# One whole-array state product in a chunked scan, its outputs gathered into one group per head pair, and two heads taken in turn

## The chip, the cores and the metric

The kernel runs on one core of a Trainium2 chip. Five engines work from queues of their own: TensorE (PE; its weight loads are listed as PEld), VectorE (DVE), ScalarE (ACT), GpSimd (POOL) and SyncE (SP), which issues the DMAs. The metric is the device time of one execution in microseconds; lower is better.

## The reference

A decoder block over 512 tokens and 1024 channels. The part that the change touches is the RWKV-7 recurrence, here for 8 heads of 64 channels:

```python
def step(state, inp):
    r_t, w_t, k_t, v_t, a_t, b_t = inp
    sa = jnp.einsum('bhvk,bhk->bhv', state, a_t)
    state = state * w_t[:, :, None, :] + sa[..., None] * b_t[:, :, None, :] + v_t[..., None] * k_t[:, :, None, :]
    y = jnp.einsum('bhvk,bhk->bhv', state, r_t)
    return state, y
```

Around it stand a projection to all branches (`u = h @ w_in`), a stick-breaking attention branch, sigmoid gates that merge both branches, an output projection, a squared-ReLU MLP and a gated embedding. All of it is float32.

## The kernel before

Large products are split into high and low parts, three matmuls for one (`mm3`, L191 to L193: 128x512 each). A "unit" is one block of weights, 8 such triples.

The program falls into stages. First comes attention, until about 176 us. Then the recurrence is worked in chunks of 64 tokens, two heads (a head pair `hp`) at a time, with 64 channels of one head on partitions 0 to 63 and of the other on 64 to 127. `prepare(hp)` makes everything of a pair that needs no state: scores within chunks (L778), the inverse of a triangular matrix by 32x32 and 64x64 pieces (L808 to L892), and transposes. `scan(hp)` then goes through the 8 chunks in order. In each chunk L919 multiplies the state `S` (both heads on the diagonal of a 128x128 tile), DVE adds it to `UV0` (L920), L928 makes the product for the next state, one matmul per head, L940 the output within the chunk, one per head, and ACT copies that output to `y` (L941); DVE (L936) forms the next `S`. After 8 chunks a normalisation of `y` follows on DVE and ACT (L953 to L960), then transposes and the gate (L965, L970).

The loop over `st` drives `prepare(st)`, `scan(st - 1)` and a list of filler units (`FILL[st]`, `mm3` products of other branches) together: `drive` takes steps of them in turn by the counts given. A scheduler then puts each engine's instructions in a fixed order; what an engine meets first in that order, it waits for. So a pair's scan runs beside the next pair's `prepare` in the stages of 208 to 360 us, and the last scan runs beside filler alone, until about 413 us. Behind it stand the up projection, output projection, MLP and embedding stages.

A matmul names rows of the array by the partitions of its inputs and columns by the partitions of its output: L928 and L940 read 128 rows and fill 64 columns, L778 reads 64 rows and fills 128 columns, L881 is 64 by 64, L871 32 by 32; L919 and the filler use the whole array. The profile shows each float32 matmul of a small product as two MATMUL instructions.

Of the kernel before, what the change touches and what calls it, by code (L numbers as in the profile page):

```python
# [14 lines left out]
ALU = mybir.AluOpType  # L15
# [3 lines left out]
P = 128  # L19
# [4 lines left out]
C = 64  # L24
NC = T // C
CP = NC // 2
# [59 lines left out]
def tile_block(ctx: ExitStack, tc: tile.TileContext, xT, xt, pT, wts, lora, cols_d, gfin_d, consts_d, out, dbg=None):  # L86
    nc = tc.nc
    act, dve, pool, pe, sync = nc.scalar, nc.vector, nc.gpsimd, nc.tensor, nc.sync

    HALVES = (slice(0, 64), slice(64, 128))  # L90
# [181 lines left out]
    with ExitStack() as sA:  # L272
# [43 lines left out]
        with ExitStack() as s1:  # L316
# [12 lines left out]
            ps = ps_z()  # L329
# [197 lines left out]
            for _ in islice(v, 1):  # L527
# [6 lines left out]
                              op0=ALU.mult, op1=ALU.add)  # L534
# [37 lines left out]
        with ExitStack() as s2:  # L572
# [22 lines left out]
            def ps_gen():  # L595
                return ps2.tile([P, T], F32, name="ps_g", bufs=3)
# [26 lines left out]
            def ps_chain():  # L623
                return ps2.tile([P, T], F32, name="ps_c", bufs=2)
# [56 lines left out]
            def prepare(hp, got):  # L681
# [90 lines left out]
                for g in range(2):  # L772
                    yield
                    pss = [ps_gen() for _ in range(2)]
                    for c in range(4):
                        cp, q = g * 2 + c // 2, c % 2
                        for hh, sl in enumerate(HALVES):
                            pe.matmul(pss[hh][:, c * P:(c + 1) * P], BK[sl, 2 * cp + 1 - q, :, :].rearrange("p s t -> p (s t)"),  # L778
                                      Q[sl, cp, 1 + 2 * q:3 + 2 * q, :], start=True, stop=True)
                    for hh in range(2):  # L780
                        ps4 = pss[hh].rearrange("p (cp s t) -> p cp s t", cp=2, s=4)
                        pk = slice(hh * 4 + 2 * g, hh * 4 + 2 * g + 2)
                        dve.tensor_tensor(out=LM[:, pk], in0=ps4[:, :, 1:3, :],
                                          in1=strict.rearrange("p (o u t) -> p o u t", o=1, u=1).broadcast_to([P, 2, 2, C]),
                                          op=ALU.mult)
                        dve.tensor_tensor(out=DE[:, hh, g * 4:g * 4 + 4, :].rearrange("p (cp q) t -> p cp q t", q=2),
                                          in0=ps4[:, :, 0::3, :],
                                          in1=incl.rearrange("p (o u t) -> p o u t", o=1, u=1).broadcast_to([P, 2, 2, C]),
                                          op=ALU.mult)
# [77 lines left out]
                ps = ps_gen()  # L867
                ps3 = ps[:, 0:256].rearrange("p (k x) -> p k x", k=8)
                for k in range(8):
                    for r in (0, 2):  # L870
                        pe.matmul(ps3[QUADS[r], k], Yc[QUADS[r + 1], k, :], Z[QUADS[r + 1], k, QUADS[r + 1]], start=True, stop=True)  # L871
                for r in (0, 2):
                    act.copy(out=Z[QUADS[r], :, QUADS[r + 1]], in_=ps3[QUADS[r]])
                yield
# [2 lines left out]
                for cp in range(CP):  # L877
                    for hh in range(2):
                        j = cp * 2 + hh
                        for q, (own, oth) in enumerate((HALVES, HALVES[::-1])):  # L880
                            pe.matmul(ps[own, j * C:(j + 1) * C], LM[oth, hh * 4 + cp, q, :], Vt[oth, cp, hh * C:(hh + 1) * C],  # L881
                                      start=True, stop=True)
                act.copy(out=MA[:, :, 0:C], in_=ps.rearrange("p (j x) -> p j x", j=8))
                yield
                UV0 = p2.tile([P, CP, 2, C], F32, name="UV0", tag="mid", bufs=NMID)
# [18 lines left out]
            def scan(hp, got):  # L904

                csl = slice(hp * P, (hp + 1) * P)
                Q, DE, UV, UV0, BKt, gc_, bon = (got[n] for n in ("Q", "DE", "UV", "UV0", "BKt", "gc_", "bon"))
                y = p2.tile([P, CP, P], F32, name="y", tag="gn", bufs=2)
                S = None
                for c in range(NC):  # L910
                    yield
                    cp, q = c // 2, 1 - c % 2
                    half, oth = HALVES[q], HALVES[1 - q]
                    psu = ps_chain()
                    if S is None:
                        pool.tensor_copy(out=UV[half, cp, q, :], in_=UV0[half, cp, :, :].rearrange("p h x -> p (h x)"))
                    else:

                        pe.matmul(psu[:, 0:P], Q[:, cp, 4 * q:4 * q + 2, :].rearrange("p s t -> p (s t)"), S, start=True, stop=True)  # L919
                        dve.tensor_tensor(out=UV[half, cp, q, :], in0=psu[half, 0:P],  # L920
                                          in1=UV0[half, cp, :, :].rearrange("p h x -> p (h x)"), op=ALU.add)
                    if c < NC - 1:
                        gc = gc_[:, c:c + 1]
                        ps = ps2.tile([P, T], F32, name="ps_s", bufs=1)
                        Sn = Sb[hp % 2 * 3 + c % 3]
                        for hh in range(2):
                            sl = HALVES[hh]
                            pe.matmul(ps[sl, 0:C], BKt[:, c, sl], UV[:, cp, q, sl], start=True, stop=True)  # L928
                        if S is None:
                            for sl in HALVES:  # L930
                                dve.tensor_scalar(out=Sn[sl, sl], in0=ps[sl, 0:C], scalar1=gc[sl], scalar2=None, op0=ALU.mult)
                        else:
                            Sg = p2.tile([P, C], F32, name="Sg", bufs=4)
                            for sl in HALVES:
                                pool.tensor_scalar(out=Sg[sl], in0=S[sl, sl], scalar1=gc[sl], scalar2=None, op0=ALU.mult)
                                dve.scalar_tensor_tensor(out=Sn[sl, sl], in0=ps[sl, 0:C], scalar=gc[sl], in1=Sg[sl],  # L936
                                                         op0=ALU.mult, op1=ALU.add)
                    for hh in range(2):
                        sl = HALVES[hh]
                        pe.matmul(psu[oth, sl], DE[:, hh, 2 * cp + q, :], UV[:, cp, q, sl], start=S is None, stop=True, skip_group_check=True)  # L940
                    act.copy(out=y[oth, cp, :], in_=psu[oth, 0:P])  # L941
                    if c < NC - 1:
                        S = Sn

                yield

                y3 = y.rearrange("p c (h x) -> p (c h) x", h=2)
                st = p2.tile([P, 4, 8], F32, name="st", bufs=2)

                def each(i):  # L950
                    return st[:, i, :].rearrange("p (j o) -> p j o", o=1).broadcast_to([P, 8, C])

                dve.tensor_reduce(out=st[:, 0, :], in_=y3, axis=mybir.AxisListType.X, op=ALU.add)  # L953
                dve.scalar_tensor_tensor(out=y3, in0=each(0), scalar=-1.0 / C, in1=y3, op0=ALU.mult, op1=ALU.add)
# [25 lines left out]
            for st in range(HP + 1):  # L980
                parts = [(len(FILL[st]) * KT, filling(FILL[st]))]
                if st < HP:
                    parts.append((28, prepare(st, got[st])))
                if st > 0:
                    parts.append((11, scan(st - 1, got[st - 1])))
                drive(*parts)


# [363 lines left out]
```

## Time and profile before

| | us |
|---|---|
| median of 3 runs | 879.9 (879.37 to 880.65) |
| the profiled execution | 881.98 |
| its span | 880.1 |
| PE busy | 860.2 (98%) |
| DVE busy | 676.5 (77%) |
| ACT busy | 452.9 (51%) |

The span is the time from the first to the last instruction of the profiled execution; 1.9 us lie around it. Busy time is a union of the instructions' durations. Matmuls are pipelined, each listed from its issue to its end, so what a matmul costs PE is read from the distance between starts, not from its duration.

### The profile page before, as it was taken

The numbers are of one execution on the slowest core, as the hardware profiler recorded it, in microseconds if no ns is written. First come the engines' busy times: TensorE is split into PE (matmuls) and PEld (weight loads), VectorE is DVE, ScalarE is ACT, GpSimd is POOL, SyncE is SP. The second block draws the span as 40 slices with busy tenths as digits, with TensorE's granted clock in tenths as the row PEclk, the third lists the DMA queues.
The fourth block names the chain that finished last, engine by engine and source line by source line (L and its number), as shares of the span: only waits on it lengthen the run. The fifth ranks groups of instructions, "written<-read, shape, count | busy, mean of one in ns | idle before, by whom it ended". The sixth has DMA issues, their size and how long they took to land.

```text
span 880.1 us, 13611 instructions
## 1 busy us (share of the span) xinstructions
PE 860.2 (98%) x5238; PEld 692.7 (79%) x5238; DVE 676.5 (77%) x1230; ACT 452.9 (51%) x730; POOL 87.3 (10%) x136
## 2 busy tenths in 40 slices
PE   8999999999999999999999999999999999999995
PEld 5778787877777777777888888888888888888885
DVE  6899987896979889456853789857975987697666
ACT  6788887734445254424523555334534543453743
POOL 1332421002302141120000000000000000000000
PEclk9999999999999999999999999999999999999998
DMA  7212212121211315238934820631252034200422
GB/s 266 97 48 73 72 61 90 66 97 50 72 50 49 109 64 173 89 132 273 307 103 135 294 73 4 202 128 50 72 189 98 25 122 165 96 1 1 168 72 96
DMA packets 32272, 95.32 MB, mean 108 GB/s; under 512 B 3664, under 2 KB 3664, under 8 KB 32208
## 3 DMA queue, kind: packets, MB, share of 16 engines
q1 hardware_dynamic: 32208, 94.46, 31.7%
q8 instruction: 41, 0.67, 0.3%
q14 instruction: 23, 0.19, 0.1%
HBM read 83.96 MB, written 10.49 MB: 107 GB/s over the span
## 4 chain that ended last, share of the span: by engine, by line
PE 77%; DVE 11%; ACT 6%; DMA 3%; issue 2%; SPq 0%; ACTq 0%; DVEq 0%
PE ps_m L191 14%; PE ps_m L192 14%; PE ps_m L193 14%; PE ps_m L206 7%; PE ps_m L208 7%; PE ps_m L207 7%; DMA w_raw<-in_wts_dram 2%; DVE w_lo L176 1%; ACT hx L1025 1%; PE ps_o L492 1%; DMA tmp<-gates 1%; PE ps_g L778 1%; PE ps_g L808 1%; PE ps_g L892 1%; PE ps_z L500 1%
## 5 line engine op out<-in xcount | busy, mean ns | idle before, releaser
L175 ACT CAST w_hi<-w_raw 128x1024 fp32r<-128x1024 f32 x94 | 98.9, 1053 | 150.2 <-PE ps_m L192 93.4
L176 DVE TENSOR_TENSOR w_lo<-w_raw,w_hi 128x1024 fp32r<-128x1024 f32 x94 | 115.3, 1226 | 37.2 <-ACT w_hi L175 36.5
L191 PE MATMUL ps_m<-h_hi,w_hi 128*128 128x512 f32 x320 | 131.3, 412 | 1.6 <-ACT w_hi L221 1.4
L192 PE MATMUL ps_m<-h_lo,w_hi 128*128 128x512 f32 x320 | 128.5, 402 | 0.3 <-DVE h_lo L349 0.3
L193 PE MATMUL ps_m<-h_hi,w_lo 128*128 128x512 f32 x320 | 128.2, 400 | 0.0
L191 PE MATMUL ps_m<-hx,w_hi 128*128 128x512 f32 x256 | 99.8, 390 | 0.4 <-ACT hx L1025 0.4
L192 PE MATMUL ps_m<-hx,w_hi 128*128 128x512 f32 x256 | 99.7, 390 | 0.0
L193 PE MATMUL ps_m<-hx,w_lo 128*128 128x512 f32 x256 | 99.6, 390 | 0.0
L191 PEld LDWEIGHTS ps_m<-h_hi,w_hi 128*128 128x128 f32 x320 | 60.6, 189 | 13.8 <-ACT w_hi L221 1.9
L193 PEld LDWEIGHTS ps_m<-h_hi,w_lo 128*128 128x128 f32 x320 | 60.2, 188 | 12.3
L192 PEld LDWEIGHTS ps_m<-h_lo,w_hi 128*128 128x128 f32 x320 | 60.4, 189 | 12.0 <-DVE h_lo L349 1.3
L191 PEld LDWEIGHTS ps_m<-hx,w_hi 128*128 128x128 f32 x256 | 48.0, 188 | 10.5 <-ACT hx L1025 0.6
L192 PEld LDWEIGHTS ps_m<-hx,w_hi 128*128 128x128 f32 x256 | 48.1, 188 | 10.1 <-DVE hx L1026 0.2
L193 PEld LDWEIGHTS ps_m<-hx,w_lo 128*128 128x128 f32 x256 | 48.1, 188 | 9.9
L208 PE MATMUL ps_m<-w_hi,fS 128*128 128x512 f32 x128 | 49.8, 389 | 0.0
L206 PE MATMUL ps_m<-w_hi,fS 128*128 128x512 f32 x128 | 49.8, 389 | 0.0
L207 PE MATMUL ps_m<-w_lo,fS 128*128 128x512 f32 x128 | 49.8, 389 | 0.0
L208 PE MATMUL ps_m<-w_hi,fA 128*128 128x512 f32 x96 | 37.4, 389 | 0.0
L206 PE MATMUL ps_m<-w_hi,fA 128*128 128x512 f32 x96 | 37.4, 389 | 0.0
L207 PE MATMUL ps_m<-w_lo,fA 128*128 128x512 f32 x96 | 37.4, 389 | 0.0
L221 ACT CAST fS<-sums 128x256 fp32r<-128x256 f32 (+1 forms) x32 | 19.8, 620 | 33.3 <-DVE sums L1117 33.3
L1190 DVE TENSOR_TENSOR xs<-ps_m,xs 128x512 f32<-128x512 f32 x56 | 35.9, 682 | 0.0
(378 smaller groups left out, 1900.2 us busy)
## 6 DMA issues: line engine op xcount, KB each, us to landing
w_raw<-in_wts_dram SPq DMA_DIRECT2D x98, 512.0 KB, 3.5
gates<-gg SPq DMA_DIRECT2D x16, 256.0 KB, 2.0
x_in<-in_xT_dram SPq DMA_DIRECT2D x8, 256.0 KB, 6.1
tmp<-gates SPq DMA_DIRECT2D x8, 256.0 KB, 3.3
upsb<-tmp SPq DMA_DIRECT2D x8, 256.0 KB, 3.2
ga<-upsb SPq DMA_DIRECT2D x8, 256.0 KB, 6.1
gb<-gates SPq DMA_DIRECT2D x8, 256.0 KB, 6.3
xs<-in_xt_dram SPq DMA_DIRECT2D x4, 512.0 KB, 6.9
```

The lines of the kernel that those rows point to most:

```text
L175: act.copy(out=hi, in_=raw)
L176: dve.tensor_tensor(out=lo, in0=raw, in1=r32(hi), op=ALU.subtract)
L191: pe.matmul(ps, wh, xh[:, k, t], start=first, stop=False)
L192: pe.matmul(ps, wh, xl[:, k, t], start=False, stop=False)
L193: pe.matmul(ps, wl, xh[:, k, t], start=False, stop=last)
L206: pe.matmul(ps, xh[:, k + j], wh, start=first and j == 0, stop=False, skip_group_check=True)
L207: pe.matmul(ps, xh[:, k + j], wl, start=False, stop=False, skip_group_check=True)
L208: pe.matmul(ps, xl[:, k + j], wh, start=False, stop=last and j == 1, skip_group_check=True)
L221: act.copy(out=hi, in_=src)
L492: pe.matmul(ps_o[:, j * P:T], vv[:, j, hh, :, :].rearrange("p a d -> p (a d)"), part[:, ZB[j]:ZB[j] + ZN[j]], start=j == 2 and part is wh, ...
L500: pe.matmul(zt[b][:, :n], tri, part[:, s:s + n], start=False, stop=False, skip_group_check=True)
L1190: dve.tensor_tensor(out=xb, in0=pss[t2], in1=xb, op=ALU.add)
```

## The change

The two state matmuls of a chunk (one per head) become one over all 128 rows and 128 columns, of which the two diagonal 64x64 blocks are used. The outputs within chunks leave the chunk loop: two PSUM banks `psy`, one for odd and one for even chunks, hold the state's part of all chunks, and after the loop 16 matmuls add to them in one group, odd and even chunk in turn; two ACT copies then fetch `y`. The scores are issued in an order that is fixed, one head after the other (`tc.issue_after`), as are the pieces of L871 before those of L881.

```diff
-                        for hh, sl in enumerate(HALVES):
-                            pe.matmul(pss[hh][:, c * P:(c + 1) * P], BK[sl, 2 * cp + 1 - q, :, :].rearrange("p s t -> p (s t)"),
-                                      Q[sl, cp, 1 + 2 * q:3 + 2 * q, :], start=True, stop=True)
+                        for hh in (1, 0):
+                            sl = HALVES[hh]
+                            with tc.issue_after(last.ins) if last else nullcontext():
+                                last = pe.matmul(pss[hh][:, c * P:(c + 1) * P], BK[sl, 2 * cp + 1 - q, :, :].rearrange("p s t -> p (s t)"),
+                                                 Q[sl, cp, 1 + 2 * q:3 + 2 * q, :], start=True, stop=True)
...
-                    for r in (0, 2):
-                        pe.matmul(ps3[QUADS[r], k], Yc[QUADS[r + 1], k, :], Z[QUADS[r + 1], k, QUADS[r + 1]], start=True, stop=True)
+                    for r in (2, 0):
+                        last = pe.matmul(ps3[QUADS[r], k], Yc[QUADS[r + 1], k, :], Z[QUADS[r + 1], k, QUADS[r + 1]], start=True, stop=True)
...
-                            pe.matmul(ps[own, j * C:(j + 1) * C], LM[oth, hh * 4 + cp, q, :], Vt[oth, cp, hh * C:(hh + 1) * C],
-                                      start=True, stop=True)
+                            with tc.issue_after(last.ins):
+                                pe.matmul(ps[own, j * C:(j + 1) * C], LM[oth, hh * 4 + cp, q, :], Vt[oth, cp, hh * C:(hh + 1) * C],
+                                          start=True, stop=True)
...
+                psy = [ps_chain() for _ in range(2)]
                 for c in range(NC):
...
-                    psu = ps_chain()
+                    psu = psy[c % 2][:, cp * P:(cp + 1) * P]
...
-                        pe.matmul(psu[:, 0:P], Q[:, cp, 4 * q:4 * q + 2, :].rearrange("p s t -> p (s t)"), S, start=True, stop=True)
+                        pe.matmul(psu, Q[:, cp, 4 * q:4 * q + 2, :].rearrange("p s t -> p (s t)"), S, start=c in (1, 2), stop=True,
+                                  skip_group_check=True)
...
-                        for hh in range(2):
-                            sl = HALVES[hh]
-                            pe.matmul(ps[sl, 0:C], BKt[:, c, sl], UV[:, cp, q, sl], start=True, stop=True)
+                        pe.matmul(ps[:, 0:P], BKt[:, c, :], UV[:, cp, q, :], start=True, stop=True)
...
-                    for hh in range(2):
-                        sl = HALVES[hh]
-                        pe.matmul(psu[oth, sl], DE[:, hh, 2 * cp + q, :], UV[:, cp, q, sl], start=S is None, stop=True, skip_group_check=True)
-                    act.copy(out=y[oth, cp, :], in_=psu[oth, 0:P])
...
+                for cp in range(CP):
+                    for hh, sl in enumerate(HALVES):
+                        for odd in (1, 0):
+                            with tc.issue_after(last.ins) if last else nullcontext():
+                                last = pe.matmul(psy[odd][HALVES[odd], cp * P + hh * C:cp * P + (hh + 1) * C], DE[:, hh, 2 * cp + 1 - odd, :],
+                                                 UV[:, cp, 1 - odd, sl], start=False, stop=True, skip_group_check=True)
+                for odd in range(2):
+                    act.copy(out=y[HALVES[odd]], in_=psy[odd].rearrange("p (c x) -> p c x", c=CP)[HALVES[odd]])
```

How the order on PE moves, at three places. In the changed kernel L919 is L926, L928 is L935, L940 is L953, L778 is L782, L871 is L875, L881 is L886 and L965 is L977. The order counts a float32 matmul once. First, PE in one chunk of the last scan, before:

```order
L919 MATMUL ps_c<-S_1573,Q 128x128
L191 MATMUL ps_g<-osb,w_hi 128x512
L192 MATMUL ps_g<-osb,w_hi 128x512
L193 MATMUL ps_g<-osb,w_lo 128x512
L191 MATMUL ps_g<-osb,w_hi 128x512
L928 MATMUL ps_s<-UV,BKt 64x64 x2
L940 MATMUL ps_c<-UV,DE 64x64 x2
```

and the same chunk in the changed kernel:

```order
L926 MATMUL ps_c<-S_1573,Q 128x128
L191 MATMUL ps_g<-osb,w_hi 128x512
L192 MATMUL ps_g<-osb,w_hi 128x512
L193 MATMUL ps_g<-osb,w_lo 128x512
L191 MATMUL ps_g<-osb,w_hi 128x512
L935 MATMUL ps_s<-UV,BKt 128x128
```

As many filler matmuls stand between the state's two products as before; the four 64-column matmuls have become one. At the end of each scan now stands one row `L953 MATMUL ps_c<-UV,DE 64x64 x16`, which in the last scan 41 filler matmuls follow before L977.

Second, PE at the scores of the second head pair, before:

```order
L764 MATMUL ps_g<-cst,Q 128x128 x4
L778 MATMUL ps_g<-Q,BK 128x128 x16
L919 MATMUL ps_c<-S_1568,Q 128x128
L192 MATMUL ps_m<-h_lo,w_hi 128x512
L193 MATMUL ps_m<-h_hi,w_lo 128x512
```

and now:

```order
L764 MATMUL ps_g<-cst,Q 128x128 x4
L782 MATMUL ps_g<-Q,BK 128x128
L192 MATMUL ps_m<-h_lo,w_hi 128x512
L926 MATMUL ps_c<-S_1568,Q 128x128
L193 MATMUL ps_m<-h_hi,w_lo 128x512
L191 MATMUL ps_m<-h_hi,w_hi 128x512
L782 MATMUL ps_g<-Q,BK 128x128 x8
L935 MATMUL ps_s<-UV,BKt 128x128
L192 MATMUL ps_m<-h_lo,w_hi 128x512
L193 MATMUL ps_m<-h_hi,w_lo 128x512
L191 MATMUL ps_m<-h_hi,w_hi 128x512
L192 MATMUL ps_m<-h_lo,w_hi 128x512
```

The 16 score matmuls stood in one row; now they stand in three, of 1, 8 and 7, with whole-array work between. Within a row the two heads now alternate; before, four of one head often followed each other.

Third, PE at the end of the triangular inverse of that pair, before:

```order
L871 MATMUL ps_g<-Z,LX 32x32
L881 MATMUL ps_g<-Vt,LM 64x64 x4
L871 MATMUL ps_g<-Z,LX 32x32 x15
L881 MATMUL ps_g<-Vt,LM 64x64 x12
L965 MATMUL ps_c<-cst,y 128x128 x4
```

and now:

```order
L875 MATMUL ps_g<-Z,LX 32x32 x16
L886 MATMUL ps_g<-Vt,LM 64x64 x16
L193 MATMUL ps_m<-h_hi,w_lo 128x512
L191 MATMUL ps_m<-h_hi,w_hi 128x512
L192 MATMUL ps_m<-h_lo,w_hi 128x512
L977 MATMUL ps_c<-cst,y 128x128
```

The 64x64 matmuls no longer stand between the 32x32 ones.

## Rows read from the trace of the kernel before

**Rows 1.** Page, part 1: busy us (share of the span) x instructions of each engine.

```profile
PE 860.2 (98%) x5238; PEld 692.7 (79%) x5238; DVE 676.5 (77%) x1230; ACT 452.9 (51%) x730; POOL 87.3 (10%) x136
```

**Rows 2.** Busy time by stretch, the stages of the scan: us, busy of each engine, clock, DMA.

```profile
208.00:260.00 52.00, 51.32 (x571) 39.28 (x570) 45.00 (x114) 24.63 (x47) 13.38 (x16) 1.00 0.18 62
260.00:312.00 52.00, 51.52 (x569) 39.73 (x565) 44.51 (x115) 23.66 (x46) 10.75 (x16) 1.00 0.20 67
312.00:360.00 48.00, 46.60 (x533) 35.46 (x532) 41.28 (x106) 23.55 (x42) 11.45 (x13) 1.00 0.41 133
360.00:402.00 42.00, 41.97 (x228) 32.66 (x227) 21.34 (x39) 12.22 (x21) 7.96 (x13) 1.00 0.38 126
```

**Rows 3.** Timeline of PE in one chunk of the last scan: start us, us, what.

```profile
380.77 0.39 PE L193 MATMUL ps_m<-h_hi,w_lo 128*128 128x512 f32 x1
381.00 0.38 PE L919 MATMUL ps_c<-S,Q 128*128 128x128 f32 x2
...
381.45 0.39 PE L192 MATMUL ps_m<-h_lo,w_hi 128*128 128x512 f32 x1
...
381.92 0.39 PE L191 MATMUL ps_m<-h_hi,w_hi 128*128 128x512 f32 x1
382.24 0.34 PE L928 MATMUL ps_s<-UV,BKt 128*64 128x64 f32 x4
382.41 0.40 PE L940 MATMUL ps_c<-UV,DE 128*64 128x64 f32 x4
382.74 0.50 PE L192 MATMUL ps_m<-h_lo,w_hi 128*128 128x512 f32 x1
383.08 0.40 PE L193 MATMUL ps_m<-h_hi,w_lo 128*128 128x512 f32 x1
```

**Rows 4.** Groups of PE instructions by line: count, busy us, mean ns, idle before.

```profile
L940 PE MATMUL ps_c<-UV,DE 128*64 128x64 f32 x128 | 12.9, 224 | 0.0
L928 PE MATMUL ps_s<-UV,BKt 128*64 128x64 f32 x112 | 9.7, 246 | 0.4 <-DVE UV L920 0.3
```

**Rows 5.** Timeline of PE at the last chunk, which has no state product.

```profile
402.23 0.39 PE L191 MATMUL ps_g<-osb,w_hi 128*128 128x512 f32 x1
...
402.55 0.45 PE L940 MATMUL ps_c<-UV,DE 128*64 128x64 f32 x4
...
403.26 0.39 PE L193 MATMUL ps_g<-osb,w_lo 128*128 128x512 f32 x1
```

**Rows 6.** L778 alone in two stretches of the first pair's scores.

```profile
178.62:179.17 0.55, 0.55 (x4) 0.55 (x5) 1.00 0.72 291
179.17:180.18 1.01, 1.01 (x20) 1.01 (x18) 1.00 0.10 20
```

**Rows 7.** Timeline of PE at the end of the second pair's inverse.

```profile
253.58 0.24 PE L871 MATMUL ps_g<-Z,LX 32*32 32x32 f32 x2
...
254.13 0.69 PE L871 MATMUL ps_g<-Z,LX 32*32 32x32 f32 x30
254.75 0.92 PE L881 MATMUL ps_g<-Vt,LM 64*64 64x64 f32 x24
255.59 0.66 PE L965 MATMUL ps_c<-cst,y 128*128 128x128 f32 x4
```

**Rows 8.** All waits of DVE for another engine, 262 to 304 us: total, times, longest.

```profile
DVE st L953 <- ACT y L941: 0.6, 1, 0.6
DVE LM L783 <- PE ps_g L778: 0.4, 1, 0.4
DVE bon L741 <- PE ps_g L637: 0.3, 1, 0.3
DVE S L936 <- PE ps_s L928: 0.2, 1, 0.2
```

**Rows 9.** End of the last scan in the timeline, and a copy from the groups.

```profile
413.78 0.63 PE L965 MATMUL ps_c<-cst,y 128*128 128x128 f32 x4 [1.72 <-DVE y L960]
...
L513 ACT COPY oo<-ps_o 64x512 f32<-64x512 f32 x4 | 2.3, 582 | 0.1
```

More of the change, by code (lines that the diff above doesn't have):

```diff
@@ L774, in prepare @@
                     pss = [ps_gen() for _ in range(2)]
+                    last = None
                     for c in range(4):
                         cp, q = g * 2 + c // 2, c % 2
-                        for hh, sl in enumerate(HALVES):
-                            pe.matmul(pss[hh][:, c * P:(c + 1) * P], BK[sl, 2 * cp + 1 - q, :, :].rearrange("p s t -> p (s t)"),
-                                      Q[sl, cp, 1 + 2 * q:3 + 2 * q, :], start=True, stop=True)
+                        for hh in (1, 0):
[3 more added lines that the diff above has]
+                                                 Q[sl, cp, 1 + 2 * q:3 + 2 * q, :], start=True, stop=True)
                     for hh in range(2):
@@ L912, in scan @@
                     cp, q = c // 2, 1 - c % 2
-                    half, oth = HALVES[q], HALVES[1 - q]
-                    psu = ps_chain()
+                    half = HALVES[q]
+                    psu = psy[c % 2][:, cp * P:(cp + 1) * P]
                     if S is None:
@@ L917, in scan @@
                     else:
-                        pe.matmul(psu[:, 0:P], Q[:, cp, 4 * q:4 * q + 2, :].rearrange("p s t -> p (s t)"), S, start=True, stop=True)
-                        dve.tensor_tensor(out=UV[half, cp, q, :], in0=psu[half, 0:P],
+                        pe.matmul(psu, Q[:, cp, 4 * q:4 * q + 2, :].rearrange("p s t -> p (s t)"), S, start=c in (1, 2), stop=True,
+                                  skip_group_check=True)
+                        dve.tensor_tensor(out=UV[half, cp, q, :], in0=psu[half],
                                           in1=UV0[half, cp, :, :].rearrange("p h x -> p (h x)"), op=ALU.add)
@@ L925, in scan @@
                         Sn = Sb[hp % 2 * 3 + c % 3]
-                        for hh in range(2):
-                            sl = HALVES[hh]
-                            pe.matmul(ps[sl, 0:C], BKt[:, c, sl], UV[:, cp, q, sl], start=True, stop=True)
+                        pe.matmul(ps[:, 0:P], BKt[:, c, :], UV[:, cp, q, :], start=True, stop=True)
                         if S is None:
                             for sl in HALVES:
-                                dve.tensor_scalar(out=Sn[sl, sl], in0=ps[sl, 0:C], scalar1=gc[sl], scalar2=None, op0=ALU.mult)
+                                dve.tensor_scalar(out=Sn[sl, sl], in0=ps[sl, sl], scalar1=gc[sl], scalar2=None, op0=ALU.mult)
                         else:
@@ L935, in scan @@
                                 pool.tensor_scalar(out=Sg[sl], in0=S[sl, sl], scalar1=gc[sl], scalar2=None, op0=ALU.mult)
-                                dve.scalar_tensor_tensor(out=Sn[sl, sl], in0=ps[sl, 0:C], scalar=gc[sl], in1=Sg[sl],
+                                dve.scalar_tensor_tensor(out=Sn[sl, sl], in0=ps[sl, sl], scalar=gc[sl], in1=Sg[sl],
                                                          op0=ALU.mult, op1=ALU.add)
-                    for hh in range(2):
-                        sl = HALVES[hh]
-                        pe.matmul(psu[oth, sl], DE[:, hh, 2 * cp + q, :], UV[:, cp, q, sl], start=S is None, stop=True, skip_group_check=True)
-                    act.copy(out=y[oth, cp, :], in_=psu[oth, 0:P])
-                    if c < NC - 1:
-                        S = Sn
+                        S = Sn
+                yield
+                last = None
+                for cp in range(CP):
[6 more added lines that the diff above has]
+                    act.copy(out=y[HALVES[odd]], in_=psy[odd].rearrange("p (c x) -> p c x", c=CP)[HALVES[odd]])
                 yield
@@ L984, in tile_block @@
                 if st > 0:
-                    parts.append((11, scan(st - 1, got[st - 1])))
+                    parts.append((12, scan(st - 1, got[st - 1])))
                 drive(*parts)
```

## The prediction

> **What bounds the kernel now.** I read the page first: PE is busy for 98% of the span and DVE for 77% [rows 1]. That says little by itself, since a busy PE may be waiting inside its own pipeline, so the next view was the busy time by stretch over the scan's stages. There the two engines are close to each other: in 208 to 260 us PE is busy for 51.32 of 52 us and DVE for 45.00, in the next stretch DVE for 44.51 of 52, in the third for 41.28 of 48; in the last, 360 to 402, DVE only for 21.34 of 42 while PE is full [rows 2]. The granted clock is 1.00 in all four, so no part of the argument rests on it. Third, the timeline of PE by starts, since what a matmul costs is the distance to the next start. Two dense filler matmuls stand 0.47 us apart (381.45 to 381.92), so one costs 0.235 us [rows 3]. Around a chunk's four L928 and four L940 instructions the starts are much further apart than these eight take: 381.92 to 383.08 is 1.16 us, and without the two filler matmuls in it 0.69 us [rows 3]. L919, which uses the whole array, costs 0.68 - 0.47 = 0.21 us by the same reading (380.77 to 381.45) [rows 3]. So 64-column work costs three times a whole-array product of twice the width. Part of it is at the edges: 0.32 us pass before the first L928 where 0.235 are due, and the first filler matmul behind takes 0.34 [rows 3]. These edges appear though the row group L928 shows almost no waiting (0.4 us over 112) [rows 4], so I read them as the price of going from the whole array to a part of it and back.
>
> **The change part by part, on PE.**
>
> *The state product.* 28 chunks have one (112 instructions in fours) [rows 4]. L928 and L940 of such a chunk cost 0.69 us; the new product has L919's form, 128 by 128 by 128, so I give it L919's 0.21 us. That is 28 x 0.48 = 13.4 us less. The four last chunks have L940 alone, 1.03 - 0.47 = 0.56 us each (402.23 to 403.26) [rows 5]: 2.2 us less.
>
> *The outputs in one group.* 32 instructions a pair. Edges: 0.085 us in, 0.105 out [rows 3]. In between, two bounds. Before, L940's two heads write the same 64 columns, and four starts lie 0.06 us apart (they last 0.40 us, one of them 0.22) [rows 3, 4]; at that pace the group costs 32 x 0.06 + 0.19 = 2.1 us. Now odd and even chunks write different columns, as L928's two heads do, whose four take 0.17 us to the next start [rows 3], and as L881's pieces, of which 24 take 0.84 us, 0.035 each [rows 7]: 32 x 0.035 + 0.19 = 1.31 us. The nearest row is L928's, with the same shape and alternation, so I take 1.31: four groups give back 5.2 us (8.4 at the other bound). The scan as a whole saves PE 13.4 + 2.2 - 5.2 = 10.4 us.
>
> The Trainium skill, "TensorE: Matmul & The Clock Gate", section on packing small matmuls, says that a weight load overlaps matmuls in flight only when its row group differs; both chunks of a pair use all rows, so by that the group would run one after another and cost about 2.1 us. The L928 rows of this case, with all rows and alternating columns, don't agree with it [rows 3].
>
> *The scores.* With one head after the other in fours, 4 instructions fill 0.55 us; alternating, 20 fill 1.01 [rows 6]: 0.14 against 0.05 us each. If some 12 of a pair's 32 now run at the slow pace, alternation saves 1.1 us. But the row of 16 is cut into three, and two more switches into a part of the array cost about 0.32 us each (the 0.56 of the last chunk without its 4 x 0.06) [rows 3, 5]. That leaves 0.45 a pair; 1.8 in all, between nothing and 4.4.
>
> *The end of the inverse.* 253.58 to 255.59 is 2.01 us [rows 7]. Without the 64x64 pieces in the middle, 32 L871 at 0.62 / 30 and 32 L881 at 0.035 make 1.78 us [rows 7]: 0.23 a pair, 0.9 in all.
>
> *By stage.* The first `prepare`: 0.45 + 0.23 = 0.7 us. Each of the three middle stages: scan 7 x 0.48 + 0.56 - 1.31 = 2.6, with the 0.7 a `prepare` saves 3.3. The last scan, beside filler alone: 2.6. PE's sum is 13.2 us.
>
> **What of it reaches the end.** In the last scan DVE has half its time free [rows 2] and the filler covers its steps, so the 2.6 us count in full, and so, beside attention's remains, do the first 0.7. In the middle stages DVE has as much to do as before: the same additions (L920) and state updates (L936), of the same shapes. From 262 to 304 us it waited for another engine for only 1.5 us in 42 [rows 8]. PE there is to become 2.6 us shorter (the first chunk's 0.48 and the inverse's 0.23 fall outside this stretch), and DVE can't follow by more than what it now waits. Bounds a stage: 0.7 us if the stretch gives nothing, 3.3 if it gives all. DVE's 1.5 lies halfway between nothing and the 2.6, and I take the middle, 2.0: 6.0 us for three stages. This is the weakest number here.
>
> *The end of the last scan.* Its normalisation can start only when the group is done and two copies have fetched it. The group costs 0.75 us more than the last chunk's L940 did, and a copy of 64x512 on ACT takes 0.58 [rows 9]; at most 0.75 + 1.16 = 1.9 us later. PE already stands idle there for 1.72 us, waiting for DVE's y at L965 [rows 9]; but about as many filler matmuls follow as before (41 in the order shown). I count nothing, with bounds of 1.7 us gained and 1.9 lost. The ACT copies saved in the chunks hide behind ACT's half-empty queue (24 of 52 us busy) [rows 2] and bring nothing. No DMA is added or moved past another; SP's share of work is as before.
>
> *Sum.* 0.7 + 6.0 + 2.6 = 9.3 us. From the profiled execution's 881.98 us that is 872.7; it stands 2.1 us above the median, so for the median 879.9 - 9.3 = 870.6 us.
>
> **The rivals.**
>
> *PE alone sets the time.* The scheduler spreads DVE's work over the gaps at the stages' borders and all of PE's 13.2 us show: 866.7. For it: DVE has 7 us free in each middle stage [rows 2]. Against it: hardly any of them in the dense stretch [rows 8].
>
> *DVE holds the middle stages.* Only 0.7 of each counts: 0.7 + 2.1 + 2.6 = 5.4, so 874.5.
>
> *The group doesn't overlap.* Then each group costs 0.8 us more, 3.3 on PE, of which two thirds show: about 873. The skill's rule on weight loads, above, would have this.
>
> *A product on the whole array is the dearer one, and the edges stay.* Half of the new product's output is thrown away. If what surrounds L928 were paid for any small product, only the starts inside would count: 0.17 + 0.24 of a chunk against 0.21 and an eighth of 32 x 0.035, so 0.06 x 28, and with scores and inverse less than 3 us in all: about 877. L919 speaks against it: it has no edge in front [rows 3]. The Trainium skill, "TensorEngine Tiling (Array Packing)", section on theoretical speedup, promises up to twice the speed where a small dimension is cut into tiles, which would argue for two products of 64 columns; L928 and L940's 0.69 us show what it leaves out here.
>
> *Waits move to PE: slower.* PE takes its work in a fixed order. It now comes to each L926 0.48 us earlier while DVE, full in the middle stages, makes S and UV no sooner. There are 56 such meetings (L926 and L935). Where each waits 0.24 us on average, all 13.2 us are gone, and above it the kernel is slower; with 0.4 us it is 9 us slower, 889. Against it: before, L928 waited 0.4 us in all [rows 4], and in the last scan there is room.
>
> **How the numbers follow.** The forecast (868.5 to 873) 0.40; PE alone 0.20; DVE holds 0.18; no overlap 0.09; edges stay 0.06; waits 0.07. The range 866 to 877 holds all but the last, and the edge of the first and fifth. About 0.2% (1.8 us) is what a measurement can tell from no change: faster 0.90, same 0.05, slower 0.05; the last two are the waits' case and the small end of the fifth.
>
> **What would show it.** By starts, L935 should cost about 0.2 us beyond the filler around it, and no filler matmul beside it 0.34. L953's 32 instructions should fill about 1.2 us; 2 us means no overlap. DVE's waits in the middle stretch should nearly vanish and PE's ahead of L926, L935 and L782 appear, together under 4 us; if they reach 10, the fifth rival is right. The last scan's stretch should be 2 to 3 us shorter. PE's idle time ahead of L977 should stay within 0 to 3.6 us. The prediction is wrong in its main step if L935 costs as much as L928 and L940 did.

## The result and the profile after

| | us |
|---|---|
| changed kernel, median of 4 runs | 875.55 (874.0 to 876.43) |
| before, median beside it | 879.92 (879.37 to 880.65) |
| ratio, 95% interval | 0.9948 [0.9931, 0.9965] |
| the profiled execution of after, its span | 875.67, 873.9 |

The change makes the kernel 4.4 us faster. The forecast was 9.3, so the time lies in the range, and the gain is less than half of what was predicted. The two profiled executions differ by 6.3 us: before's stood 2.1 above its median, and 0.9 us of the difference lies ahead of the first score matmul, in attention, which the change doesn't touch.

One line of the change is missing from the diff above: `drive` takes the scan's steps by a count of 12 instead of 11 (`parts.append((12, scan(...)))`), since the scan has one step more, a `yield` ahead of the group. The prediction didn't price it; c1 and r1 below do.

In the changed kernel the names of lines are L926 (was L919), L928 (L920, the addition that makes `UV`), L935 (L928), L938 and L943 (L931 and L936, `S`), L953 (L940), L977 (L965). First the page's part 1 of after, against [rows 1]:

```profile
PE 853.8 (98%) x5182; PEld 685.9 (78%) x5182; DVE 676.6 (77%) x1230; ACT 449.1 (51%) x706; POOL 83.7 (10%) x136
```

Then the stretches of [rows 2] in after:

```profile
208.00:260.00 52.00, 50.73 (x553) 38.25 (x552) 43.40 (x111) 24.16 (x41) 13.34 (x16) 1.00 0.19 62
260.00:312.00 52.00, 51.21 (x556) 38.91 (x556) 45.55 (x115) 22.71 (x39) 10.19 (x15) 1.00 0.22 72
312.00:360.00 48.00, 46.50 (x526) 34.58 (x525) 42.65 (x108) 21.96 (x35) 10.81 (x12) 1.00 0.39 126
360.00:402.00 42.00, 41.97 (x228) 33.75 (x228) 21.98 (x42) 13.99 (x22) 5.59 (x13) 1.00 0.51 174
```

Both views say little: PE is as full as before and DVE as loaded. A better ruler is the filler, since the same matmuls are done in both kernels. Below are the busy time and number of matmuls into `ps_m` (all filler in these stretches), with the stretches cut where the program is at the same place: the first score matmul, the first L892 (L897 in after) of each pair, and the last `y` transpose. Before:

```profile
177.10:206.00 28.90, 19.92 (x78) 1.00 0.27 93
206.00:256.90 50.90, 31.96 (x118) 1.00 0.19 64
256.90:308.20 51.30, 32.08 (x117) 1.00 0.20 68
308.20:358.10 49.90, 30.80 (x110) 1.00 0.36 118
358.10:413.70 55.60, 23.38 (x91) 1.00 0.49 164
```

and after:

```profile
176.20:206.00 29.80, 21.95 (x86) 1.00 0.27 90
206.00:255.90 49.90, 32.74 (x120) 1.00 0.20 65
255.90:306.30 50.40, 32.51 (x120) 1.00 0.22 74
306.30:358.80 52.50, 33.84 (x123) 1.00 0.38 122
358.80:407.50 48.70, 17.88 (x68) 1.00 0.53 175
```

In the last stretch there are 116 more filler matmuls, into `ps_g`, in either kernel. A filler matmul costs 0.23 us by its distance to the next. So the gain of a stretch is its shortening plus 0.23 for each filler matmul that it takes in beyond before. The view counts a matmul that crosses an edge on both sides, so the middle stages seem to take in 18 more; counted by starts it is 16. First `prepare`: -0.9 + 8 x 0.23 = 0.9. The three middle stages: 152.1 us became 152.8 with 16 matmuls more, -0.7 + 3.7 = 3.0. The last: 6.9 - 23 x 0.23 = 1.6. The forecast was 0.7, 6.0 and 2.6. The last stage is 7 us shorter to look at, mostly because filler moved out of it into earlier stages. The sum, 5.5, is 0.2 above the shortening itself (236.6 to 231.3); by starts there is one filler matmul more in after (609 against 608), and some records of matmuls can be missing. Two later runs, r6 and r5, turned out to be the same two kernels once more; read in this way they give 0.6, 2.2 and 2.0.

Where the missing part went shows in the timeline of one chunk, PE and under it DVE. Before, four filler matmuls from L928 to L919, in the second stage:

```profile
259.74 0.34 PE L928 MATMUL ps_s<-UV,BKt 128*64 128x64 f32 x4
259.90 0.40 PE L940 MATMUL ps_c<-UV,DE 128*64 128x64 f32 x4
...
261.03 0.39 PE L192 MATMUL ps_m<-h_lo,w_hi 128*128 128x512 f32 x1
261.26 0.38 PE L919 MATMUL ps_c<-S,Q 128*128 128x128 f32 x2
261.40 0.47 PE L193 MATMUL ps_m<-h_hi,w_lo 128*128 128x512 f32 x1
```

```profile
260.23 0.59 DVE L931 TENSOR_SCALAR S<-ps_s,gc__2158 64x64 f32<-64x64 f32 x2
```

After, with the same four filler matmuls between:

```profile
208.72 0.39 PE L935 MATMUL ps_s<-UV,BKt 128*128 128x128 f32 x2
...
209.64 0.39 PE L191 MATMUL ps_m<-h_hi,w_hi 128*128 128x512 f32 x1
210.04 0.46 PE L926 MATMUL ps_c<-S,Q 128*128 128x128 f32 x2
210.26 0.48 PE L192 MATMUL ps_m<-h_lo,w_hi 128*128 128x512 f32 x1
```

```profile
209.31 0.59 DVE L938 TENSOR_SCALAR S<-ps_s,gc__1651 64x64 f32<-64x64 f32 x2
```

Before, `S` is ready at 260.82 and L919 starts at 261.26: it comes 0.44 us later than it must. L940 and its edges are part of those 0.44 us; they stand between the state's product and the next read of the state, where DVE makes `S`. After, they are gone, `S` is ready at 209.90, and L926 starts at 210.04, which is 0.40 behind the filler matmul ahead of it where 0.23 is due. From the state's product to the next L926 the chunk now takes 1.32 us instead of 1.52: of the 0.48 us of PE work taken out of a chunk, 0.20 shows here. The 0.44 us aren't all won, because `S` itself comes later behind the product's start (1.18 us where it was 1.08) and L926 follows `S` by 0.14: 0.44 - 0.10 - 0.14 = 0.20. No idle time is listed for L926, because the filler matmul ahead still runs to its listed end while L926 waits.

The same over all meetings, worked out from the starts and ends in the trace: in the middle stages (206 to 359 us) before, L919 starts 0.47 us (median of 21) after the end of the last `S` step, and one of them within 0.06; after, the median for L926 is 0.06, and 12 of 21 start within 0.06. Between filler matmuls (from the start of the one before to the start of the second one behind, less two fillers of 0.229), L919 cost 0.233 us on average in the middle stages (13 of them, none over 0.30; two others, next to other small products, did wait, 1.1 us together by the view of waits); L926 costs 0.43 (15, of which 13 over 0.30), and L935 0.37 (10, half of them over 0.30).

The waits of PE from 170 to 420 us in after, from the longest (us in total, times, longest), show only the tip:

```profile
PE ps_c L977 <- DVE y L972: 2.1, 1, 2.1
PE ps_g L831 <- DVE tmp L827: 1.9, 4, 0.8
PE ps_g L875 <- ACT LX L869: 0.6, 1, 0.6
PE ps_c L926 <- DVE S L943: 0.3, 2, 0.2
```

Last, the rows that answer to [rows 3] and [rows 9] in the timeline of PE: a group of outputs, a meeting without a wait, and the end of the last scan.

```profile
241.36 0.40 PE L192 MATMUL ps_m<-h_lo,w_hi 128*128 128x512 f32 x1
241.69 1.15 PE L953 MATMUL ps_c<-UV,DE 128*64 128x64 f32 x32
242.77 0.50 PE L193 MATMUL ps_m<-h_hi,w_lo 128*128 128x512 f32 x1
243.11 0.40 PE L191 MATMUL ps_m<-h_hi,w_hi 128*128 128x512 f32 x1
...
365.83 0.40 PE L193 MATMUL ps_m<-h_hi,w_lo 128*128 128x512 f32 x1
366.07 0.38 PE L935 MATMUL ps_s<-UV,BKt 128*128 128x128 f32 x2
366.21 0.48 PE L191 MATMUL ps_m<-h_hi,w_hi 128*128 128x512 f32 x1
366.52 0.39 PE L192 MATMUL ps_m<-h_lo,w_hi 128*128 128x512 f32 x1
...
407.55 0.63 PE L977 MATMUL ps_c<-cst,y 128*128 128x128 f32 x4 [2.12 <-DVE y L972]
```

L935 costs 366.52 - 365.83 - 0.47 = 0.22 us here, and the 32 instructions of L953 with their edges 243.11 - 241.36 - 0.47 = 1.28.

### The profile page after: what moved, and what is told of

Its sections match the earlier page's. It is cut to its first block, busy times and chain, and to the rows that moved or that the text cites. A ratio compares the mean times of both kernels' runs of the same rounds, so it can differ in the third digit from the quotient of the medians.

```text
span 873.9 us, 13420 instructions
## 1 busy us (share of the span) xinstructions
PE 853.8 (98%) x5182; PEld 685.9 (78%) x5182; DVE 676.6 (77%) x1230; ACT 449.1 (51%) x706; POOL 83.7 (10%) x136
## 4 chain that ended last, share of the span: by engine, by line
PE 70%; DVE 16%; ACT 7%; DMA 3%; issue 2%; SPq 0%; ACTq 0%; DVEq 0%
PE ps_m L191 13%; PE ps_m L193 13%; PE ps_m L192 12%; PE ps_m L208 7%; PE ps_m L206 7%; PE ps_m L207 7%; DVE w_lo L176 3%; DMA w_raw<-in_wts_dram 1%; ACT hx L1037 1%; ACT w_hi L175 1%; PE ps_o L492 1%; PE ps_g L897 1%; DVE LX L835 1%; PE ps_z L500 1%; PE ps_c L926 1%
```

## The experiments

Two theories stood after the result. **Meetings**: PE's work shrank as costed, but what it saved is waited for again where PE meets DVE's `S` and `UV` (the fifth rival's mechanism, at a size that leaves a gain). **DVE's load**: DVE has no time left in the middle stages (the second rival). A third was added by the count of 12: **order** alone, since any edit of the program moves what stands where.

### The parts alone

e1 is the changed scan (its count too) with the scores and inverse of before; e2 and e3 are before with the scores, or the inverse's order, of the change; e9 is the change with the scores of before; e10 is before with the scores and the inverse. Each takes over the piece of the diff shown above, as in e9:

```diff
-                        for hh in (1, 0):
-                            sl = HALVES[hh]
-                            with tc.issue_after(last.ins) if last else nullcontext():
...
+                        for hh, sl in enumerate(HALVES):
```

> The change to the scan alone (one state product, outputs in one group); scores and inverse as before. PE does about 7.5 us less around state and output than before. If VectorE binds the middle stages: 3 to 5 us faster than before, nearly all of what the whole change brought (4.4). If the scores' new order is what cost the missing time (its three rows, a first prepare 1 us longer): 6 to 9 us faster than before, so better than the whole change.

> Only the scores of two heads in turn. By the sum on TensorE 1.8 us faster. If VectorE binds: within 0.7 us of before. If the split into three rows costs: 1 to 3 us slower.

> Only the order of the 32x32 and 64x64 pieces at the end of the inverse. TensorE saves 0.23 us in each of four prepares: 0.9 us faster if that end is a chain of TensorE and ScalarE on which the stage hangs; nothing if VectorE binds.

> The changed kernel with the scores' order of before: scan and inverse changed. Alone they brought 3.2 and 3.1 us. If parts add up except where VectorE's chain takes over: 4 to 5 us faster than before, as the whole change. If the split of the scores into three rows is what the whole change loses by: 6 us or more.

> Scores and inverse changed, the scan as before. Alone they brought 2.8 and 3.1 us. If each takes its gain from the same slack: 3 to 4.5 us faster than before. If they add up: 6 us.

| | median us | ratio to before [95%] |
|---|---|---|
| e1 scan | 877.18 | 0.9963 [0.9948, 0.9977] |
| e2 scores | 877.57 | 0.9966 [0.9954, 0.9979] |
| e3 inverse | 877.32 | 0.9960 [0.9945, 0.9976] |
| e9 scan and inverse | 875.97 | 0.9959 [0.9946, 0.9973] |
| e10 scores and inverse | 877.61 | 0.9968 [0.9958, 0.9979] |

Each alone gives about 3 us, the whole change 4.4. The three parts don't add up, and e3, which takes 0.9 us of PE's work away by the forecast, gives 3.1 between the medians (3.5 by the ratio). That can't be its own work alone; the controls below show what else it is. One thing does follow the scan's part: from starts (the rule stands at the last table), the 28 L919 cost 6.8, 7.1 and 8.0 us in e2, e3 and e10, where the scan is that of before, and 8.5 in before; the 28 L926 cost 10.3 and 11.6 in e1 and e9, where the scan is changed, and 10.0 in the whole change.

### The product alone

```diff
-                        for hh in range(2):
-                            sl = HALVES[hh]
-                            pe.matmul(ps[sl, 0:C], BKt[:, c, sl], UV[:, cp, q, sl], start=True, stop=True)
+                        pe.matmul(ps[:, 0:P], BKt[:, c, :], UV[:, cp, q, :], start=True, stop=True)
```

> Only the whole-array state product; the outputs stay behind it in each chunk. If the edges between whole array and part of it are what the change saves, they stay here (one in, one out a chunk): within 1.5 us of before. If the whole-array product is itself the gain, 28 x 0.48 less what L940 costs alone, 0.56 a chunk: 28 x (0.69 - 0.56 - 0.14), about nothing as well, but if the product is the dearer form, as its wasted half says: 1 to 3 us slower.

Measured 883.01 us, 1.0024 [1.0014, 1.0034]: slower, by 2.1 us by the ratio and 2.6 between the medians. The timeline of PE in a chunk, with the outputs (here L938) still in the loop:

```profile
260.69 0.40 PE L191 MATMUL ps_m<-h_hi,w_hi 128*128 128x512 f32 x1
260.93 0.38 PE L926 MATMUL ps_s<-UV,BKt 128*128 128x128 f32 x2
261.24 0.45 PE L938 MATMUL ps_c<-UV,DE 128*64 128x64 f32 x4
261.62 0.50 PE L192 MATMUL ps_m<-h_lo,w_hi 128*128 128x512 f32 x1
261.95 0.39 PE L193 MATMUL ps_m<-h_hi,w_lo 128*128 128x512 f32 x1
```

The chunk costs 261.95 - 260.69 - 0.47 = 0.79 us against 0.69 before [rows 3]: the product is cheap, but the edges stay with the outputs, which cost 0.56 alone [rows 5]. 28 x 0.10 is 2.8 us, near what was measured, though partly by luck: from starts all 28 chunks together cost 4.7 us more (0.87 us each against 0.70), and L919 1.0 less than in before. So the whole-array product pays only together with moving the outputs out. The Trainium skill, "TensorEngine Tiling (Array Packing)", section on key properties, says that a change of tiling mode drains TensorE; these rows agree, and give the price here. And with L940's work left where it was, L919 hardly waits: in the middle stages the median cost between fillers is 0.227 us (14 of them, 13 under 0.30), as in before. The whole-array product by itself makes no wait for `S`; taking the outputs' cover away does. Its own wait for `UV` is another matter: with the cover left, 8 of the 28 products of e4 start within 0.07 us of the end of the step that makes `UV`, and these cost 0.43 to 0.68 us, where one that doesn't wait costs 0.32 (260.93 to 261.24, above).

### The group one chunk after the other

All odd chunks first, then all even, so that neighbours fill the same columns:

```diff
-                for cp in range(CP):
-                    for hh, sl in enumerate(HALVES):
-                        for odd in (1, 0):
+                for odd in (1, 0):
+                    for cp in range(CP):
+                        for hh, sl in enumerate(HALVES):
```

> The changed kernel with all odd chunks of the output group first, then all even ones, so that neighbours fill the same columns. TensorE needs about 0.8 us more per group (2.1 against 1.3). If TensorE's time counted in full: 3 us slower than the changed kernel, so 1.5 us faster than before. If VectorE binds the middle: about 1 us slower than the changed kernel, from the last scan alone.

Measured 876.76 us, 0.9950 [0.9931, 0.9969]. One group in its timeline:

```profile
241.56 1.90 PE L953 MATMUL ps_c<-UV,DE 128*64 128x64 f32 x32
```

1.90 us against 1.15: alternating columns are worth 0.75 us a group, 3.0 in all on PE, of which 1.2 show in the medians, within what the intervals can't tell apart. In the profiled execution PE's idle time ahead of L977 is 0.2 us, against 2.1 in after and 1.0 in r5, so part of the 3.0 is probably taken out of that wait. Both forms use all rows. The Trainium skill, "TensorE: Matmul & The Clock Gate", section on packing small matmuls, lets a weight load overlap matmuls in flight only where the row group differs; by that the two forms would cost the same, and these rows don't agree with it.

### Less DVE work, more DVE work

e5 (changed kernel) and e6 (before) leave out the low part of the weights of 16 gate units on DVE and use the high part in its place. r3 (changed) and r4 (before) add 64 multiplies, written as two in each of the 32 chunks, whose output nothing uses.

```diff
-            dve.tensor_tensor(out=lo, in0=raw, in1=r32(hi), op=ALU.subtract)
+            if seq[i][0] in (U_GSB, U_GRW):
+                lo = hi
+            else:
+                dve.tensor_tensor(out=lo, in0=raw, in1=r32(hi), op=ALU.subtract)
```

```diff
+                    junk = p2.tile([P, 256], F32, name="junk", bufs=1)
+                    for _ in range(2):
+                        dve.tensor_tensor(out=junk, in0=t13[:, 0:256], in1=t13[:, 256:512], op=ALU.mult)
```

> The changed kernel without VectorE's low part (1.21 us each) for the 16 gate units, 2 to 6 of them in a stage, 19 us in all; TensorE multiplies by the high part a second time instead, so its work is the same. This leaves out accuracy of the gates. If VectorE's load binds the middle stages: TensorE's saved time now shows, and the kernel is 5 us or more faster than the changed one, so 10 us or more faster than before. If the waits come from the fixed order and from latencies alone: at most 2 us faster than the changed kernel.

> The same left out of the kernel before. If VectorE binds there only when TensorE is made shorter: at most 3 us faster than before, so that the distance to the run above (the worth of the change without VectorE in the way) is 8 us or more. If the distance stays near 4.4 us, VectorE's load isn't what holds the change back.

> The changed kernel with two extra DVE multiplies of 128x256 in each of the 32 chunks (some 26 us of DVE, about 6.5 a stage; their output is used by nothing). Theory A (DVE's steps end last in the middle stages): most of what three stages get shows, 10 to 20 us. Theory B (only the order): DVE's free 6 to 8 us a stage take it in, 0 to 5 us.

> The same extra DVE work in the kernel before. Theory A: PE ended last there in most of a stage, so clearly less shows than in the changed kernel: 4 to 6 us less of it, and the change is then worth about nothing. Theory B: as much as in the changed kernel, within 2 us, and the change is still worth some 4 us.

Measured: e5 874.48, 0.9920 [0.9898, 0.9942]; e6 880.75, 1.0002 [0.9985, 1.0018]; r3 877.96, 0.9967 [0.9951, 0.9984]; r4 882.48, 1.0024 [1.0011, 1.0037]. Page, part 1, of r3 (r4 has DVE at 698.0):

```profile
PE 854.7 (98%) x5182; PEld 685.7 (78%) x5182; DVE 698.1 (80%) x1294; ACT 449.6 (51%) x706; POOL 86.1 (10%) x136
```

21.5 us more on DVE (698.1 against 676.6) cost both kernels 2.4 us, and about 16 us less gave the changed one 1.1 (2.5 by the ratios) and the other nothing. But the multiplies didn't run in their chunks: nothing ties them to a chunk, and in r3 they start between 144.8 and 264.2 us. Below are their busy time and number in r3 ahead of the scores, in the first `prepare` and in the first middle stage (one more starts behind it), and a wait that r3 and r4 have and after and before haven't:

```profile
140.00:179.00 39.00, 7.53 (x18) 1.00 0.22 75
179.00:213.50 34.50, 12.24 (x29) 1.00 0.28 93
213.50:264.00 50.50, 6.75 (x16) 1.00 0.20 65
```

```profile
PE ps_g L637 <- DVE tmp L633: 1.8, 1, 1.8
```

The 2.4 us were lost ahead of the scan, where this wait lies: the first score matmul starts at 179.0 us in both, against 176.2 in after and 177.1 in before. So r3 loads only the first middle stage. There DVE is busy for 49.0 of 50.5 us (43.4 of 49.9 in after), and PE's time beyond the filler (the stage less 0.23 for each filler matmul that starts in it) is 22.0 us against 22.5: no loss. e5 answers for the other two: DVE is busy for 39.0 of 48.4 and 37.5 of 49.0 us there, against 44.0 of 50.4 and 44.1 of 52.5, and PE's time beyond the filler in the three stages is 70.1 us against 70.0: no gain. DVE's load is not what holds the gain back: the second rival falls. Nor do the extra loads, where they ran, make L919 wait in before: it still costs 0.226 (median of 13 in r4) where L926 costs 0.43 (median of 14) in r3.

### Order alone

c1 sets only the scan's count in before to 12, r1 sets it in the changed kernel back to 11; c2 and r2 set `prepare`'s count to 26 in before and in the changed kernel; e8 sets the scan's count in the changed kernel to 18. No work changes.

```diff
-                    parts.append((11, scan(st - 1, got[st - 1])))
+                    parts.append((12, scan(st - 1, got[st - 1])))
```

> A control: the kernel before with the scan driven at 12 in place of 11 steps, as the changed kernel drives it; no instruction is added or removed, only the fixed order differs. If order alone matters little: within 1 us of before. If the missing and the extra microseconds of the single parts come from the order: 1.5 us or more off, either way.

> A second control of that kind: the kernel before with prepare driven at 26 in place of 28. Same expectations: within 1 us, or 1.5 us and more off.

> The changed kernel with the scan's count 11 instead of 12 in the drive of scan, next prepare and filler; same work, another order. Theory A (the rest of PE's gain is lost because DVE's steps now end last in the middle stages): 874.5 to 877, since no order takes DVE's work away. Theory B (it is lost to the particular order that the scheduler happened to give): another order moves it by up to 2 us either way, as the same edit of counts in the kernel before did (2.1 us less), and some order comes near 872.

> The changed kernel with the prepare's count 26 instead of 28; same work, another order. Theory A: 874.5 to 877. Theory B: up to 2 us either way, near 872 to 873 if the order was what kept the gain back; the kernel before gained 2.1 us by the same edit.

> The changed kernel with the scan driven sooner against prepare (18 in place of 12), so that its normalisation and the transposes of y (split around the inverse's last product in the changed kernel, where VectorE then sits 4.4 us behind ScalarE's yf in each middle stage) end before the stage's border. If that wait is what eats the gain: 5 us or more faster than the changed kernel. If VectorE's load binds anyway or the state chain gets in TensorE's way: the same within 1.5 us, or slower.

| | median us | ratio to before [95%] |
|---|---|---|
| c1 before, scan 12 | 878.0 | 0.9974 [0.9964, 0.9984] |
| c2 before, prepare 26 | 877.95 | 0.9973 [0.9963, 0.9983] |
| r1 changed, scan 11 | 876.02 | 0.9953 [0.9937, 0.9969] |
| r2 changed, prepare 26 | 873.85 | 0.9925 [0.9903, 0.9948] |
| e8 changed, scan 18 | 875.55 | 0.9948 [0.9930, 0.9965] |

Two other orders of the same work make the kernel before 2 us faster: its own order is an unlucky one. The traces show part of what is unlucky about it. Waits of PE from 170 to 420 us, first two in before, then one in c2 and one in r2:

```profile
PE ps_c L919 <- DVE S L936: 1.1, 2, 0.6
PE ps_g L827 <- DVE tmp L823: 0.3, 1, 0.3
PE ps_g L827 <- DVE tmp L823: 1.6, 4, 0.5
PE ps_g L831 <- DVE tmp L827: 0.4, 1, 0.4
```

L919's wait in before is gone in c1 and c2: from starts, its 28 cost 8.5 us in before and 6.7 in either, and the end of the inverse 9.1 against 7.8 and 8.0. L919 is cheaper in e2 and e3 too (6.8 and 7.1), so a good part of the 3 us that e1 to e3 each gave is probably this; e1 is only 0.8 us better than c1, which has its count. The wait at L831 (L827), on the other hand, comes and goes with the order in either kernel. With equal counts the change is worth 4.1 us at 11 (880.1 to 876.02) and 2.4 at 12 (878.0 to 875.55); the fastest order tried of each kernel, c2 and r2, lie 4.1 apart. None of these comes near 9. In all four orders of the change L926 waits in the middle stages (median cost between fillers 0.39, 0.41, 0.47 and 0.33 us), and in none of the three of before does L919 by that median (0.227, 0.226, 0.228). r2 is the fastest of all, 1.7 us below the change; their intervals overlap. e8 took DVE's wait for `yf` from 12.7 us to 2.4 (170 to 420 us) and gained nothing by it.

### Less filler

> The changed kernel with 48 filler matmuls fewer, of 0.235 us each, in the three middle stages (the product of h's low part with the high part of the weights is left out for six gate units, two a stage): 11.3 us of PE that stand at no meeting with another engine. Theory P (PE's time, waits and edges included, is the end in both kernels, and the missing part of the gain went into new small waits of PE): nearly all of it shows, 9.5 to 11.3 us less than the changed kernel. Theory C (in the middle stages chains through several engines are the end, so that PE time saved there shows by half only, whatever is saved): 4 to 7 us less.

> The same 48 filler matmuls left out of the kernel before. Theory P: 9.5 to 11.3 us less than before. Theory C: 4 to 7 us less, or, if only the changed kernel has come to that limit, 9.5 to 11.3 here against 4 to 7 there.

```diff
-        pe.matmul(ps, wh, xl[:, k, t], start=False, stop=False)
+        if lo:
+            pe.matmul(ps, wh, xl[:, k, t], start=False, stop=False)
```

The edit took no effect: `mm3` binds `lo` again, to the low part of the weights, so all 48 matmuls were still done, and the pages count 5182 and 5238 matmuls on PE as without it. The two are repeats of the kernels themselves, 875.05 us at 0.9934 [0.9919, 0.9949] and 879.84 at 0.9993 [0.9982, 1.0003], and confirm the result. What PE time taken out of the filler would give is left open.

## Why the prediction was half right

**The costs on PE held.** L935 costs 0.22 us where it doesn't wait (0.21 forecast). L953's 32 instructions took 1.28 us with their edges, against 1.31. The two matters that could have gone against the change on PE, no overlap and edges that stay, didn't come; e7 and e4 show both prices where they do apply.

**The step that failed is "what of it reaches the end", for the three middle stages.** The forecast gave 6.0 us there, 2.0 a stage, and called it the weakest number; they gave 3.0 (2.2 in the repeats), so about 1.0 a stage between the bounds of 0.7 and 3.3. The bounds held, the middle between them did not. That the time, 875.55, lies nearest to the second rival's 874.5 is chance, since the cause that it names is not the one. The reason given, DVE's load, is not the cause (r3 and e5 above): what counts is how long DVE's steps take from one product of a chunk to the next, not how full DVE is. What takes the larger part are the meetings, the fifth rival's mechanism: worked out from starts, the time to the next start put to each instruction and a filler's excess over 0.229 to the small product beside it (the one behind, where there are two), PE's time over the scan changed so, in after against before and in r2 against c2, the fastest order tried of each kernel:

| | forecast | after less before | r2 less c2 |
|---|---|---|---|
| state's product and outputs, with edges and waits at L935 | -10.4 | -7.5 | -7.5 |
| L926 | 0 | +1.5 | +3.7 |
| scores | -1.8 | -0.8 | +0.1 |
| end of the inverse | -0.9 | -0.7 | -0.5 |
| L831 | 0 | +1.8 | -0.5 |
| all else | 0 | +0.5 | +0.3 |

With the excess put to the product ahead instead, rows of the first pair move by up to 0.8 and of the second by up to 1.5; L926 stays at 1.0 and 3.6.

28 L935 cost 0.33 us each, not 0.21, or 3.3 us in all. Nine of them start within 0.07 us of the end of the step that makes `UV` and hold 2.1 us of that; six next to score and other small matmuls, which cost 0.33 to 0.42 without such a wait, hold 0.9. L926's 1.5 is measured against an order in which L919 itself waited; against c2 it is 3.7. L831's 1.8 is not a price of the change: the same wait stands in c2 and hardly in r2. The scores, too, gave less than their 1.8, in r2 nothing. The argument against the fifth rival, that L928 hardly waited before [rows 4], failed: it looked at another meeting. What L940 covered, standing behind L928, was L919's wait for `S`; and the whole-array product pays more for its waits for `UV` than L928 did, with L940 still in its place: 8 of 28 in e4 cost 2.0 us above 0.32 each, 7 of 28 in before 0.7 above 0.26. The rival's price was right in kind and too high in size (0.24 us for each of 56 meetings; 2.1 + 1.5 us in after, and 2.5 + 3.7 in r2 against c2, are 0.06 and 0.11), so a gain was left.

**The last scan** gave 1.6 instead of 2.6. DVE's free half did not cover everything: three of six L935 between fillers cost over 0.30 us there, and PE's idle time ahead of L977 is 2.12 us against 1.72 [rows 9], within the bounds given for it. That these 0.4 us are a loss isn't shown: in r5 and r6, the same two kernels, it is 1.0 and 0.9, and the last scan gave 2.0 there. **The first `prepare`** gave 0.9 (0.7 forecast).

**What was to show it.** The sign by which the prediction was to be wrong (L935 as dear as L928 and L940) didn't come. "PE's waits ahead of L926, L935 and L782 together under 4 us" looks right in the view of waits, which lists 0.6 us, and is wrong by the starts: the waiting L935 hold 2.1 us, and the 28 L926 cost 3.6 more than at 0.227 each.

Still open: what in the order of before makes L919 wait where its neighbours don't, and whether one more filler matmul between L935 and L926, or outputs put there for some chunks, would win the rest back. Neither was tried.

## What to carry to other kernels

Before work is taken from an engine with a fixed order, look at what that work covers: read, in the kernel before, the distance from the end of the producer's step on the other engine to the start of the consumer (here 0.44 us behind `S`, of which 0.20 were won), and count as gain no more than that distance unless other work moves in. Don't rely on listed idle time for it: where matmuls overlap, a wait of up to some 0.2 us shows only in the distance between starts. And give a change of a few tenths of a per cent a control that moves only the order: here one was worth 2 us, as much as half the change. Where work is added as a test, look in the trace for where it ran: the multiplies of r3 and r4 had left most of their chunks.

## What was not expected of the hardware

A whole-array product that is followed at once by products on 64 columns pays the edge all the same: in e4 0.31 us pass from L926 to L938 (260.93 to 261.24), where 0.14 pass from L935 to a filler matmul (366.07 to 366.21). And a float32 product of two instructions that had to wait takes longer by more than the wait: its pair lasts 0.46 us where it waited (L926 at 210.04) and 0.38 where it didn't (L919 at 261.26), so its second instruction starts 0.08 us later behind the first. The wait alone isn't the reason: L935 at 225.10, right behind score matmuls and 0.94 us after its `UV`, also takes 0.24 us to the next start, where 0.14 is the rule. What the reason is, no run shows.
